# Three value projections between the RWKV projections, and other memory for the retention's tiles

## The chip, the cores and the metric

The kernel runs on one core of one Trainium2 chip. The metric is the device time of one execution, in microseconds (us). The kernel before the change takes 1903.56 us, the median of 3 runs (1901.87 to 1906.99).

## What is computed

A decoder block on 1024 tokens of width 1024, all in float32. One projection of the normalised input feeds two token mixers and two gates; the mixers' outputs are merged, and a feed-forward part with a short convolution follows:

```python
hn = rms_norm(h, norm_mix_pre);  p = hn @ w_in
p_rw, p_ret, g_rw, g_ret = split(p)        # 1792, 3072, 1024, 1024 columns
y_rw  = rwkv7_mixer(p_rw, ...)             # r, k, v, decay, a, g; a recurrence per head
y_ret = retention_mixer(p_ret, positions)  # q, k, v, g; 8 heads, chunks of 128 tokens
merged = sigmoid(g_rw) * (y_rw @ w_branch_rw) + sigmoid(g_ret) * (y_ret @ w_branch_ret)
h = h + rms_norm(merged @ w_out, norm_mix_post)
h = h + rms_norm(conv_ffn(rms_norm(h, norm_ffn_pre), ...), norm_ffn_post)
```

The retention works chunk by chunk: scores of a chunk against itself under a decay mask, plus the query times a carried state, then a normalisation per head and a product with the gate.

## The kernel before

A framework orders the instructions: it takes the program in the order written as the priority, simulates the engines, and gives each engine a fixed list. What is written inside a `high_priority` block counts as written 500 instructions earlier; weight loads (`load_w`) and the emptying of PSUM are in such blocks. Memory comes from pools that are stacked on the left or the right end of SBUF. A pool that is opened where another was closed waits, tile by tile, for the last use of what lay there.

Every large product is done as three matmuls per 128 rows (`mm3`): both operands are split into a high and a low float32r part, and high x high, high x low and low x high are added up in PSUM. `load_w` brings in 512 KB of weights on SP's queue, casts the high part on ScalarE (line 211) and subtracts for the low part on VectorE when a running count is divisible by 3, otherwise on GpSimd (line 216).

The 54 column tiles of `w_in` (128 columns each, 1024 tokens in two halves of 512) fall into two kinds. Tiles 0 to 13 are the RWKV ones: `rw_tiles` and `rw_tile` (lines 339 to 367) project them, and VectorE and ScalarE mix each with its shifted self. Four come first; then a loop over i = 0 to 3 (lines 402 to 464) computes decay and `a` from two small products (`p_lw`, `p_a`), scans, scales k and r, and writes the packed operands of the recurrence to DRAM (`L_d`). The others are the side tiles: `qk_pair` projects q and k with their rotation (tiles 14 to 21), `side_tile(i)` v (22 to 29), the retention's gate (30 to 37) and the two merge gates (38 to 53). Both put their result through the PSUM tag "a" (two banks, which the RWKV tiles use too) and the buffer `ot` into the DRAM tensor `pj_d`:

```python
w = load_w(wch[i], 8)
for hf in range(2):
    ps = psA.tile([128, 512], F32, tag="a", name="ps_side")
    proj(w, ps, hf)                                   # 24 matmuls of 512 columns
    with tc.high_priority(offset=WPRIO):
        ot = gp.tile([128, 512], F32, tag="ot", name="ot")
        if i < 30:
            S.copy(ot, ps)
```

In program order there follow: the recurrence, 8 chunks (lines 576 to 762), its memory (`rc`, `r1`, `r2`) on the right; the side tiles up to 37; the retention (`first_stage` of chunk j+1, then `second_stage` of chunk j); the side tiles 38 to 53; the first product of the RWKV branch (`ps_b0`, 8 x 12 matmuls, lines 881 to 897), from `yrw_d` and the gates in `pj_d`; then the merge for two halves of the tokens, whose second product (`ps_b`, lines 998 to 999) takes the retention's output `yret_d`.

The retention's pool `t2` is opened on the right when the recurrence's pools are closed. A chunk's q, k, v and gate come in one load `zvg` (1.5 MB, two buffers, SP's queue); `vt`, `sm`, `kt_`, `R`, `on` and `yr` have two buffers each, and `yr` goes out in one store on ScalarE's queue. `t2` is closed behind the retention; `h2`, `np` (the first product's gates `gt0`, tag "pr") are opened then in its place, and `mr` (the product's inputs) on the left. The rotation's tables `cosT` and `sinT` lie in `hp`, as does the projections' input `hn`.

Of the kernel before, what the change touches and what calls it, by code (L numbers as in the profile page):

```python
# [158 lines left out]
def body(tc, nc, xT, xN, pos, wch, wbrw, wbret, wout, wup, wdn, w2a2, gw2, rows, vecs, consts0, consts1, out):  # L159
# [3 lines left out]
    @contextmanager  # L163
    def tile_pool(**kw):
        with tc.tile_pool(**kw) as pool:
            yield Lines(pool)

    with ctx:
# [101 lines left out]
        cosT = hp.tile([128, T], F32, name="cosT")  # L270
        sinT = hp.tile([128, T], F32, name="sinT")
# [44 lines left out]
        def rbh(hf):  # L316
            return rbT[:, 512 * hf:512 * hf + 512]

# [7 lines left out]
        with pctx, tile_pool(name="p1", bufs=1, reuse_waits="tile", side="right") as p1:  # L326
# [57 lines left out]
            rt, rg, k0, r0 = rw_tiles([(12, "v_"), (13, "cs"), (4, "k_"), (0, "r_")], w0)  # L384
            nc.sync.dma_start(cst[1], consts1)
# [16 lines left out]
            for i in range(4):  # L402
# [58 lines left out]
                for c in range(2):  # L461

                    o = 2048 + 128 * i + 64 * (1 - c)
                    nc.scalar.dma_start(L_d[:, :, o:o + 64].rearrange("j p t -> p j t"), v_.rearrange(jct, c=2, t=64)[:, :, c, :])

# [34 lines left out]


        pj_d = dp.tile([40, 128, T], F32, name="pj_d")

        def qk_pair(m):

            ws = [load_w(wch[14 + 2 * m + e], 8) for e in range(2)]
            for hf in range(2):
                h_ = slice(hf * 512, (hf + 1) * 512)
                ab = []
                for e in range(2):  # L510
                    ps = psA.tile([128, 512], F32, tag="a", name="ps_side")
                    proj(ws[e], ps, hf)
                    with tc.high_priority(offset=WPRIO):
                        t = gp.tile([128, 512], F32, tag=f"qk{e}", name="qk", bufs=1)
                        S.copy(t, ps)
                    ab.append(t)
                a_, b_ = ab
                o1 = gp.tile([128, 512], F32, tag="ot", name="ot")
                t2 = gp.tile([128, 512], F32, tag="rt", name="rot", bufs=1)
                G.tensor_tensor(out=o1, in0=a_, in1=cosT[:, h_], op=ALU.mult)  # L520
                V.tensor_tensor(out=t2, in0=b_, in1=sinT[:, h_], op=ALU.mult)
                V.tensor_tensor(out=o1, in0=o1, in1=t2, op=ALU.subtract)
                G.tensor_tensor(out=a_, in0=a_, in1=sinT[:, h_], op=ALU.mult)
                V.tensor_tensor(out=b_, in0=b_, in1=cosT[:, h_], op=ALU.mult)
                o2 = gp.tile([128, 512], F32, tag="ot", name="ot")
                V.tensor_tensor(out=o2, in0=b_, in1=a_, op=ALU.add)
                dst = pj_d[2 * m:2 * m + 2, :, h_].rearrange("i (e z d) t -> z (i e) d t", e=2, z=2)
                for z, o in enumerate((o1, o2)):
                    for n in range(4):
                        nc.scalar.dma_start(dst[z, n], o[32 * n:32 * n + 32, :])  # L530

        def side_tile(i):

            w = load_w(wch[i], 8)
            for hf in range(2):
                ps = psA.tile([128, 512], F32, tag="a", name="ps_side")
                proj(w, ps, hf)
                with tc.high_priority(offset=WPRIO):
                    ot = gp.tile([128, 512], F32, tag="ot", name="ot")
                    if i < 30:  # L540
                        S.copy(ot, ps)
                    elif i < 38:
                        V.tensor_tensor(out=ps, in0=ps, in1=rbh(hf), op=ALU.mult)
# [222 lines left out]
        for i in range(22, 38):  # L766
            side_tile(i)
# [535 lines left out]
```

## Time and profile before

| | us |
|---|---|
| median of 3 runs | 1903.56 |
| the profiled execution | 1905.19 |
| its span, first to last instruction | 1903.4 |
| TensorE busy | 1789.1 |
| VectorE busy | 1194.9 |
| GpSimd busy | 697.7 |
| ScalarE busy | 648.5 |

The mean granted clock of TensorE was 0.979 of full speed. Busy time counts each engine's instructions, with overlaps of one engine counted once; a matmul's own time (0.39 us) is longer than the distance to the next, for they run pipelined. Stretches below are counted from the first instruction.

### The profile page before, as it was taken

To read this page: it belongs to the slowest core of one execution; us is meant where nothing else is said; L and a number is where in the kernel's file an instruction comes from. 1 tells how busy PE (TensorE), PEld (TensorE's weight loads), DVE (VectorE), ACT (ScalarE), POOL (GpSimd) and SP (SyncE) were. 2 spreads that over 40 slices of the span, in tenths; PEclk is the share of its full clock that TensorE was granted. 3 is DMA by queue.
4 is the path that set the end of the run, shared out by engine and by line. 5 is a ranking of instruction groups with operands and counts; after the bars stand their busy time and mean duration, and the time that the engine had idled before them with its cause. 6 is when DMAs were issued, how large, how long until landed. Compare 5 with 4: busy or idle time off the path is not lost.

```text
span 1903.4 us, 27398 instructions
## 1 busy us (share of the span) xinstructions
PE 1789.1 (94%) x10610; PEld 1451.0 (76%) x10610; DVE 1194.9 (63%) x2052; ACT 648.5 (34%) x993; POOL 697.7 (37%) x507
## 2 busy tenths in 40 slices
PE   8779999999999999999999999788999999999996
PEld 7657778788777778878788777666777777778885
DVE  4786584755666634663445828879888887753413
ACT  6543211111111112332443434543443444443330
POOL 1344523312212111111564744746455445222533
PEclk9989989999999999999999999899999999999998
DMA  8333532433333225555743726332222222674531
GB/s 289 90 106 100 191 81 68 133 90 94 109 93 111 69 78 162 154 178 172 238 155 119 241 89 194 133 132 104 80 78 78 78 78 75 213 221 142 178 102 44
DMA packets 202691, 244.44 MB, mean 128 GB/s; under 512 B 60993, under 2 KB 136257, under 8 KB 201537
## 3 DMA queue, kind: packets, MB, share of 16 engines
q1 hardware_dynamic: 125712, 171.11, 29.0%
q10 hardware_dynamic: 76848, 71.59, 11.5%
q8 instruction: 83, 1.36, 0.3%
q14 instruction: 48, 0.39, 0.1%
HBM read 177.10 MB, written 65.54 MB: 127 GB/s over the span
## 4 chain that ended last, share of the span: by engine, by line
PE 53%; DVE 23%; DMA 9%; issue 5%; ACT 5%; POOL 3%; ACTq 1%; SPq 0%; DVEq 0%; POOLq 0%
PE ps_side L223 7%; PE ps_side L222 7%; PE ps_side L224 7%; DVE u_f L1059 4%; PE ps_dn L224 3%; PE ps_dn L223 3%; PE ps_dn L222 3%; DVE u_f L1061 2%; POOL w_lo L1153 2%; DVE w_sa L1157 2%; DVE w_sa L1156 1%; PE ps_o L223 1%; PE ps_o L224 1%; PE ps_o L222 1%; PE ps_b L224 1%
## 5 line engine op out<-in xcount | busy, mean ns | idle before, releaser
L216 POOL TENSOR_TENSOR w_lo<-w_st,w_hi 128x1024 fp32r<-128x1024 f32 (+2 forms) x107 | 251.0, 2347 | 483.0 <-ACT w_hi L211 156.1
L211 ACT CAST w_hi<-w_st 128x1024 fp32r<-128x1024 f32 (+2 forms) x162 | 161.7, 999 | 396.6 <-PE ps_side L223 123.0
L223 PE MATMUL ps_side<-hnl,w_hi 128*128 128x512 f32 x640 | 256.2, 400 | 0.0
L222 PE MATMUL ps_side<-hnh,w_hi 128*128 128x512 f32 x640 | 256.0, 400 | 0.0
L224 PE MATMUL ps_side<-hnh,w_lo 128*128 128x512 f32 x640 | 255.1, 399 | 0.0
L222 PEld LDWEIGHTS ps_side<-hnh,w_hi 128*128 128x128 f32 x640 | 121.1, 189 | 26.9 <-issue 1.5
L223 PEld LDWEIGHTS ps_side<-hnl,w_hi 128*128 128x128 f32 x640 | 121.2, 189 | 26.4 <-issue 1.5
L224 PEld LDWEIGHTS ps_side<-hnh,w_lo 128*128 128x128 f32 x640 | 121.1, 189 | 26.3 <-issue 0.8
L216 DVE TENSOR_TENSOR w_lo<-w_st,w_hi 128x1024 fp32r<-128x1024 f32 (+1 forms) x55 | 71.9, 1307 | 83.6 <-ACT w_hi L211 39.6
L1059 DVE SCALAR_TENSOR_TENSOR u_f<-ub,vct,u_f 128x512 f32<-128x512 f32 x88 | 102.7, 1171 | 8.2 <-ACT u_f L1058 8.1
L1153 POOL TENSOR_TENSOR w_lo<-w_st,w_hi 128x512 fp32r<-128x512 f32 (+1 forms) x53 | 105.9, 2021 | 1.4 <-issue 1.4
L1058 ACT ACTIVATE u_f<-ub,vct 128x512 f32<-128x512 f32 x76 | 59.9, 813 | 123.6 <-DVE ub L1191 102.3
L222 PE MATMUL ps_rw<-hnh,w_hi 128*128 128x512 f32 (+1 forms) x224 | 86.9, 388 | 13.4 <-ACT hnh L287 7.2
L223 PE MATMUL ps_rw<-hnl,w_hi 128*128 128x512 f32 (+1 forms) x224 | 86.1, 385 | 0.3 <-DVE hnl L288 0.3
L224 PE MATMUL ps_rw<-hnh,w_lo 128*128 128x512 f32 (+1 forms) x208 | 79.7, 384 | 0.0
L224 PE MATMUL ps_b<-y_hi,w_lo 128*128 128x512 f32 x192 | 75.7, 395 | 2.9 <-DVE w_lo L216 2.0
L222 PE MATMUL ps_b<-y_hi,w_hi 128*128 128x512 f32 x192 | 75.9, 395 | 0.2 <-ACT w_hi L211 0.2
L223 PE MATMUL ps_b<-y_lo,w_hi 128*128 128x512 f32 x192 | 75.4, 393 | 0.0
L1061 DVE SCALAR_TENSOR_TENSOR u_f<-ub,vct,u_f 128x512 f32<-128x512 f32 x88 | 72.6, 843 | 0.2
L222 PE MATMUL ps_dn<-f_k,w_hi 128*128 128x512 f32 (+1 forms) x198 | 72.4, 366 | 0.0
L224 PE MATMUL ps_dn<-f_k,w_lo 128*128 128x512 f32 (+1 forms) x198 | 72.4, 366 | 0.0
L223 PE MATMUL ps_dn<-f_k,w_hi 128*128 128x512 f32 (+1 forms) x198 | 72.2, 366 | 0.0
(419 smaller groups left out, 4376.5 us busy)
## 6 DMA issues: line engine op xcount, KB each, us to landing
w_st<-in_wup_dram SPq DMA_DIRECT2D x54, 512.0 KB, 3.5
w_st<-in_wch_dram SPq DMA_DIRECT2D x52, 512.0 KB, 4.0
w_st<-in_wdn_dram SPq DMA_DIRECT2D x38, 512.0 KB, 4.1
pj_d<-ot ACTq DMA_DIRECT2D x64, 256.0 KB, 2.2
zvg<-pj_d SPq DMA_DIRECT2D x8, 1536.0 KB, 9.0
f_d<-u_f ACTq DMA_DIRECT2D x44, 256.0 KB, 2.1
L<-L_d SPq DMA_DIRECT2D x8, 1344.0 KB, 5.8
gt<-pj_d SPq DMA_DIRECT2D x32, 256.0 KB, 4.2
```

The lines of the kernel that those rows point to most:

```text
L211: S.copy(hi, st)
L216: eng.tensor_tensor(out=lo, in0=st, in1=hi, op=ALU.subtract)
L222: PE.matmul(ps, wh, xh, start=first and a == 0, stop=False, skip_group_check=skip)
L223: PE.matmul(ps, wh, xl, start=False, stop=False, skip_group_check=skip)
L224: PE.matmul(ps, wl, xh, start=False, stop=last and a == n - 1, skip_group_check=skip)
L1058: S.activation(u, src, AF.Identity, bias=VC("cb")[:, i:i + 1], scale=VC("cw2")[:, i:i + 1])
L1059: V.scalar_tensor_tensor(out=u, in0=ub[:, 1:513], scalar=VC("cw1")[:, i:i + 1], in1=u, op0=ALU.mult, op1=ALU.add)
L1061: V.scalar_tensor_tensor(out=u, in0=ub[:, 0:512], scalar=VC("cw0")[:, i:i + 1], in1=u, op0=ALU.mult, op1=ALU.add)
L1153: eng.tensor_tensor(out=w[1][:, ks, :], in0=src, in1=w[0][:, ks, :], op=ALU.subtract)
L1156: V.tensor_tensor(out=sa[:, lh, :], in0=st2[:, lh, :], in1=st2[:, rh_, :], op=ALU.add)
L1157: V.tensor_tensor(out=sa[:, rh_, :], in0=st1[:, lh, :], in1=st2[:, lh, :], op=ALU.subtract)
```

## The change

The definitions of `qk_pair`, `side_tile` and `pj_d` move, word for word, ahead of the RWKV projections. `side_tile(22)` is written behind the first four RWKV tiles, `side_tile(23)` at the end of the loop's pass i = 0, `side_tile(24)` at the end of pass i = 1; the loop behind the recurrence starts at 25. `h2` and `np` are opened ahead of the retention, `t2` (small vectors only from now on) and `mr` on the left. The retention's large tiles go to slots of other pools: q, k, gate, `vt` and `sm` into the 16 tags of `h2`; v into the memory of `cosT` and `sinT`, over which `on` is then written; `kt_` and `R` into tags of `gp`. The gate's tile takes the product in place of `yr`. The framework's DMA scratch shrinks to 1024 bytes.

```diff
-        cosT = hp.tile([128, T], F32, name="cosT")
-        sinT = hp.tile([128, T], F32, name="sinT")
+        cosT = hp.tile([128, T], F32, tag="tb0", name="cosT")
+        sinT = hp.tile([128, T], F32, tag="tb1", name="sinT")
...
             rt, rg, k0, r0 = rw_tiles([(12, "v_"), (13, "cs"), (4, "k_"), (0, "r_")], w0)
+            n_early = (1, 1, 1, 0, 0)
+            i_early = iter(range(22, 22 + sum(n_early)))
+            for _ in range(n_early[0]):
+                side_tile(next(i_early))
...
+                for _ in range(n_early[1 + i]):
+                    side_tile(next(i_early))
...
-        for i in range(22, 38):
+        for i in range(22 + sum(n_early), 38):
             side_tile(i)
...
-        tctx = ExitStack()
-        t2 = tctx.enter_context(tile_pool(name="t2", bufs=2, reuse_waits="tile", side="right"))
+        h2 = ctx.enter_context(tile_pool(name="h2", bufs=1, reuse_waits="tile", side="right"))
+        nctx = ExitStack()
+        np_ = nctx.enter_context(tile_pool(name="np", bufs=2, reuse_waits="tile", side="right"))
+        t2 = hctx.enter_context(tile_pool(name="t2", bufs=2, reuse_waits="tile"))
+        mr = hctx.enter_context(tile_pool(name="mr", bufs=1, reuse_waits="tile"))
+
+        def slots(j, n, name):
+            return [h2.tile([128, 4, 128], F32, tag=f"b0{z}{4 * (j % 2) + n}", name=name) for z in "hl"]
...
-                zvg = t2.tile([128, 24, 128], F32, name="zvg")
-                nc.sync.dma_start(zvg, pj_d[0:24, :, tk].rearrange("i p t -> p i t"))
-            Z, vc, sg = (zvg[:, 8 * n:8 * n + 8, :] for n in range(3))
-            vt = t2.tile([128, 8, 128], F32, name="vt")
+                Z = slots(j, 0, "Z")
+                vc = hp.tile([128, 8, 128], F32, tag=f"tb{j % 2}", name="vc")
+                sg = slots(j, 1, "sg")
+                for z in range(2):
+                    nc.sync.dma_start(Z[z], pj_d[4 * z:4 * z + 4, :, tk].rearrange("i p t -> p i t"))
+                nc.sync.dma_start(vc, pj_d[8:16, :, tk].rearrange("i p t -> p i t"))
+                for z in range(2):
+                    nc.sync.dma_start(sg[z], pj_d[16:24, :, tk].rearrange("(i e) p t -> e p i t", e=2)[z])
+            vt = slots(j, 2, "vt")
...
-            sm = t2.tile([128, 8, 128], F32, name="sm")
+            sm = slots(j, 3, "sm")
...
-                kt_ = t2.tile([128, 4, 128], F32, name="kt_")
+                kt_ = gp.tile([128, 4, 128], F32, tag="rt", name="kt_", bufs=1)
...
-                R = t2.tile([128, 4, 128], F32, name="R")
+                R = gp.tile([128, 4, 128], F32, tag=f"qk{j % 2}", name="R", bufs=1)
...
-            return Z, vt, sm, sg, Rj
+            return Z, vc, vt, sm, sg, Rj
-        def second_stage(j, Z, vt, sm, sg, Rj):
-            on = t2.tile([128, 8, 128], F32, name="on")
+        def second_stage(j, Z, on, vt, sm, sg, Rj):
...
-            yr = t2.tile([128, 4, 2, 128], F32, name="yr")
...
-                V.tensor_tensor(out=yr[:, :, e, :], in0=p_y.rearrange(h4, h=4),
-                                in1=sg.rearrange("p (i e) t -> p i e t", e=2)[:, :, e, :], op=ALU.mult)
-            nc.scalar.dma_start(yret_d[:, :, j * 128:(j + 1) * 128].rearrange("(i e) p t -> p i e t", e=2), yr)
+                V.tensor_tensor(out=sg[e], in0=p_y.rearrange(h4, h=4), in1=sg[e], op=ALU.mult)
+                nc.scalar.dma_start(yret_d[:, :, j * 128:(j + 1) * 128].rearrange("(i e) p t -> e p i t", e=2)[e], sg[e])
...
-        tctx.close()
         for i in range(38, 54):
             side_tile(i)
...
-    nc = bacc.Bacc("TRN2", target_bir_lowering=False, num_devices=1)
+    nc = bacc.Bacc("TRN2", target_bir_lowering=False, num_devices=1, dynamic_dma_scratch_size=1024)
```

## Rows read from the trace of the kernel before

**Rows 1.** The page: the span, and busy us of each engine (share, instructions).

```profile
span 1903.4 us, 27398 instructions
PE 1789.1 (94%) x10610; PEld 1451.0 (76%) x10610; DVE 1194.9 (63%) x2052; ACT 648.5 (34%) x993; POOL 697.7 (37%) x507
```

**Rows 2.** Stretches: us, busy us by engine (instructions), clock, DMA share, GB/s.

```profile
57.00:212.70 155.70, 137.64 (x568) 106.84 (x569) 115.12 (x104) 67.57 (x82) 72.34 (x65) 0.93 0.35 107
90.00:104.00 14.00, 3.08 (x9) 1.77 (x8) 13.26 (x9) 3.86 (x6) 7.58 (x7) 0.66 0.43 137
146.00:182.00 36.00, 34.16 (x150) 26.83 (x148) 24.93 (x22) 14.92 (x18) 19.02 (x13) 1.00 0.31 97
182.00:212.70 30.70, 29.48 (x128) 23.25 (x129) 20.45 (x18) 10.15 (x12) 14.78 (x14) 1.00 0.41 127
212.70:720.00 507.30, 502.22 (x4603) 402.77 (x4602) 298.25 (x790) 92.54 (x145) 118.60 (x112) 0.99 0.34 99
720.00:876.00 156.00, 155.35 (x1018) 126.60 (x1017) 94.11 (x320) 45.63 (x97) 21.65 (x13) 1.00 0.52 160
905.40:926.50 21.10, 18.14 (x71) 13.45 (x70) 10.40 (x12) 8.21 (x14) 11.42 (x8) 0.94 0.76 263
```

**Rows 3.** Waits of TensorE, 57 to 212.7 us: total, times, longest.

```profile
PE p_a L414 <- ACT ta L416: 7.3, 1, 7.3
PE ps_rw L222 <- DVE v__314 L362: 5.0, 1, 5.0
PE p_lw L410 <- ACT th L412: 3.6, 1, 3.6
```

**Rows 4.** Timeline of TensorE, 83 to 105 us: start, duration, instruction.

```profile
85.67 0.40 PE L223 MATMUL ps_rw<-hnl,w_hi 128*128 128x512 f32 x1
90.46 0.39 PE L223 MATMUL ps_rw<-hnl,w_hi 128*128 128x512 f32 x1
104.22 0.63 PE L222 MATMUL ps_rw<-hnh,w_hi 128*128 128x512 f32 x1
```

**Rows 5.** Stretches, instructions of the side tiles' PSUM tile alone.

```profile
212.70:720.00 507.30, 350.01 (x1410) 261.25 (x1410) 28.87 (x42) 28.21 (x48) 0.99 0.34 99
720.00:876.00 156.00, 94.75 (x382) 69.43 (x381) 11.02 (x16) 0.00 (x0) 1.00 0.52 160
876.00:905.40 29.40, 29.40 (x131) 24.21 (x129) 3.45 (x5) 0.00 (x0) 1.00 0.64 214
```

**Rows 6.** Groups by line, 57 to 212.7 us: count, busy us, mean ns.

```profile
L216 POOL TENSOR_TENSOR w_lo<-w_st,w_hi 128x1024 fp32r<-128x1024 f32 x7 | 19.4, 2779 | 7.7 <-PE ps_rw L224 7.7
L211 ACT CAST w_hi<-w_st 128x1024 fp32r<-128x1024 f32 x10 | 10.4, 1044 | 23.0 <-DVE BKp L447 11.9 <-PE ps_rw L223 11.1
L216 DVE TENSOR_TENSOR w_lo<-w_st,w_hi 128x1024 fp32r<-128x1024 f32 x3 | 3.6, 1213 | 0.0
```

**Rows 7.** The side tiles' output tile: duration ns min/median/max, first and last start.

```profile
L541 ACT COPY ot<-ps_side x16: 571/584/587, 349.7 to 490.4; 128x512 f32<-128x512 f32 x16
```

**Rows 8.** Timeline of all engines, 96 to 101 us.

```profile
96.33 1.22 DVE L446 TENSOR_TENSOR k__316<-ta,k__316 128x1024 f32<-128x1024 f32 x1
97.55 2.35 POOL L216 TENSOR_TENSOR w_lo<-w_st,w_hi 128x1024 fp32r<-128x1024 f32 x1
97.65 3.33 DVE L447 TENSOR_TENSOR BKp<-k__316,th 128x1024 f32<-128x1024 f32 x1
```

**Rows 9.** Waits of SP's DMA queue, 700 to 930 us.

```profile
SPq L783 <- DVE yr L863: 52.4, 6, 16.6
```

**Rows 10.** DMA issues: count, KB each, median us to landing.

```profile
zvg<-pj_d SPq DMA_DIRECT2D x8, 1536.0 KB, 9.0
yret_d<-yr ACTq DMA_DIRECT2D x8, 512.0 KB, 7.1
yt<-yret_d ACTq DMA_DIRECT2D x16, 256.0 KB, 4.6
```

**Rows 11.** Instructions on the retention's output in DRAM.

```profile
L973 ACTq DMA_DIRECT2D yt<-yret_d x16: 326/326/572, 906.5 to 982.4; - x16
```

More of the change, by code (lines that the diff above doesn't have):

```diff
@@ L317, in rbh, with qk_pair @@
             return rbT[:, 512 * hf:512 * hf + 512]
+        pj_d = dp.tile([40, 128, T], F32, name="pj_d")
+        def qk_pair(m):
+            ws = [load_w(wch[14 + 2 * m + e], 8) for e in range(2)]
+            for hf in range(2):
+                h_ = slice(hf * 512, (hf + 1) * 512)
+                ab = []
+                for e in range(2):
+                    ps = psA.tile([128, 512], F32, tag="a", name="ps_side")
+                    proj(ws[e], ps, hf)
+                    with tc.high_priority(offset=WPRIO):
+                        t = gp.tile([128, 512], F32, tag=f"qk{e}", name="qk", bufs=1)
+                        S.copy(t, ps)
+                    ab.append(t)
+                a_, b_ = ab
+                o1 = gp.tile([128, 512], F32, tag="ot", name="ot")
+                t2 = gp.tile([128, 512], F32, tag="rt", name="rot", bufs=1)
+                G.tensor_tensor(out=o1, in0=a_, in1=cosT[:, h_], op=ALU.mult)
+                V.tensor_tensor(out=t2, in0=b_, in1=sinT[:, h_], op=ALU.mult)
+                V.tensor_tensor(out=o1, in0=o1, in1=t2, op=ALU.subtract)
+                G.tensor_tensor(out=a_, in0=a_, in1=sinT[:, h_], op=ALU.mult)
+                V.tensor_tensor(out=b_, in0=b_, in1=cosT[:, h_], op=ALU.mult)
+                o2 = gp.tile([128, 512], F32, tag="ot", name="ot")
+                V.tensor_tensor(out=o2, in0=b_, in1=a_, op=ALU.add)
+                dst = pj_d[2 * m:2 * m + 2, :, h_].rearrange("i (e z d) t -> z (i e) d t", e=2, z=2)
+                for z, o in enumerate((o1, o2)):
+                    for n in range(4):
+                        nc.scalar.dma_start(dst[z, n], o[32 * n:32 * n + 32, :])
@@ new lines, in side_tile @@
+        def side_tile(i):
+            w = load_w(wch[i], 8)
+            for hf in range(2):
+                ps = psA.tile([128, 512], F32, tag="a", name="ps_side")
+                proj(w, ps, hf)
+                with tc.high_priority(offset=WPRIO):
+                    ot = gp.tile([128, 512], F32, tag="ot", name="ot")
+                    if i < 30:
+                        S.copy(ot, ps)
+                    elif i < 38:
+                        V.tensor_tensor(out=ps, in0=ps, in1=rbh(hf), op=ALU.mult)
+                        S.activation(ot, ps, AF.Tanh, scale=0.5)
+                        V.scalar_tensor_tensor(out=ot, in0=ot, scalar=1.0, in1=ps, op0=ALU.add, op1=ALU.mult)
+                    else:
+                        V.tensor_tensor(out=ot, in0=ps, in1=rbh(hf), op=ALU.mult)
+                        S.activation(ot, ot, AF.Tanh, scale=0.5)
+                    nc.scalar.dma_start(pj_d[i - 14, :, hf * 512:(hf + 1) * 512], ot)
@@ L499, in body @@
                 V.tensor_tensor(out=dst, in0=dst, in1=rbT, op=ALU.mult)
[L502 to L543, printed above, removed]
-                        S.activation(ot, ps, AF.Tanh, scale=0.5)
-                        V.scalar_tensor_tensor(out=ot, in0=ot, scalar=1.0, in1=ps, op0=ALU.add, op1=ALU.mult)
-                    else:
-                        V.tensor_tensor(out=ot, in0=ps, in1=rbh(hf), op=ALU.mult)
-                        S.activation(ot, ot, AF.Tanh, scale=0.5)
-                    nc.scalar.dma_start(pj_d[i - 14, :, hf * 512:(hf + 1) * 512], ot)
@@ L799, in first_stage @@
                     lo = 64 * e
[L800 removed]
+                    PE.matmul(p_ss[e][:, i * 128:(i + 1) * 128], Z[1][lo:lo + 64, i, :], Z[0][lo:lo + 64, i, :],
                               start=True, stop=True)
             for e in range(2):
[L803 removed]
+                V.tensor_tensor(out=sm[e], in0=p_ss[e].rearrange(h4, h=4), in1=rmask, op=ALU.mult)
             Rj = R
```

16 lines of the change are left out of this document (5 added, 11 removed).

## The prediction

> **What bounds the kernel now.** I began with the page's busy times, then cut the span into stages with the stretch table, then asked in each stage what TensorE waits for. TensorE is busy 1789.1 of 1903.4 us [rows 1]; the stages tell where the rest lies [rows 2]. From 212.7 to 720 us (the RWKV recurrence) it is busy 502.22 of 507.30 us, from 720 to 876 us (the retention) 155.35 of 156.00: there the side tiles (the projections of q, k, v and the gates) fill what the two mixers leave open, and every matmul taken out shortens the stage, as long as other fillers remain. The stage before, 57 to 212.7 us, holds the RWKV projections without side tiles: busy 137.64 of 155.70 us at a granted clock of 0.93. The reader should see there that TensorE is not the bound: from 90 to 104 us it is busy 3.08 of 14 us while VectorE is busy 13.26, and the granted clock averages 0.66 of 2.4 GHz, so a part of the stretch ran at 1.2 GHz [rows 2]. The waits name the cause: 7.3 us for `ta`, 3.6 us for `th`, and, ending where the stage begins, 5.0 us for a PSUM bank that VectorE empties [rows 3].
>
> **The pace of a tile.** From 85.67 to 90.46 us, 21 matmuls of 512 columns start one behind the other: 4.79 us, or 0.228 us each [rows 4]. A side tile has 2 x 8 x 3 = 48 of them, 10.9 us; the three moved ones have 144, 32.8 us. The stage from 57 to 212.7 us holds 568 matmuls [rows 2], all 512 wide, so 129.5 us of work in 155.7: 26.2 us are free, the time lost to the half-rate clock among them.
>
> **Step 1, three tiles leave the full stage.** Taking 144 matmuls out of the stages that TensorE fills takes 32.8 us off them if fillers don't run out. The side tiles' matmuls lie 1410 in the recurrence, 382 in the retention and 131 behind it [rows 5]. If the recurrence and the retention keep their gaps, they want 1792 fillers; 37 tiles have 1776. The 16 that are short (3.6 us) come from the first branch product, 8 x 12 = 96 matmuls, which has operands of its own from now on. So I cost running short at nothing; the cover is that product, and without it the price is 3.6 us. What is late next, behind the retention, is the branch's second product (rival 2).
>
> **Step 2, three tiles enter the projection stage.** The stage then holds 712 matmuls, 162.3 us at full pace. Lower bound of its growth: 6.6 us, if no hole is left. Upper bound: 32.8 us, if VectorE's chain sets the pace and the tiles only push it along. Between them I take the filling that this stage reaches where it runs best: from 146 to 212.7 us there are 150 + 128 matmuls, 63.4 us of work in 66.7, or 0.950 [rows 2]. 162.3 / 0.950 is 170.8 us, 15.1 more than now. The big hole takes the first tile: TensorE's dense run ends just behind 90.46 us and resumes at 104.22 [rows 4], and a tile of 10.9 us placed ahead of that shifts the blocked `p_a` matmul to where `ta` is free. The other two tiles lie where only some 13 us of small holes and half-rate clock are left, so they mostly lengthen the stage. Steps 1 and 2: 32.8 - 15.1 = 17.7 us gained, with bounds 0 and 26.2.
>
> **What each moved tile brings with it.** A weight load on the SP queue, a cast on ScalarE (1.04 us), a subtraction on GpSimd (2.78 us on average) or VectorE (1.21 us) [rows 6], two copies of 0.58 us out of PSUM on ScalarE [rows 7] and two DMAs on ScalarE's queue. The engine of the subtraction goes by a count, so the load order shifts it: of the three extra ones, two fall to GpSimd and one to VectorE. ScalarE is busy 67.57 of 155.7 us, GpSimd 72.34, VectorE 115.12 [rows 2]; 3 x 2.2, 2 x 2.8 and 1.2 us fit under all of them while TensorE sets the pace, and the growth taken in step 2 (8.5 us above its floor) holds them. In the 14 us where VectorE has no room the cover is gone: there one subtraction costs its 1.2 us. The evacuations need no VectorE, and each frees its bank of the two that the RWKV tiles also use. The copy waits for its matmuls in ScalarE's queue, and `ta`, `th` and the casts stand behind it; half a tile is 5.5 us, so one badly placed copy costs at most that.
>
> A row speaks for a higher price. The `BKp` product (line 447) takes 3.33 us when it starts 0.10 us behind a weight subtraction on GpSimd, while the product of the same size on line 446 took 1.22 us just before it [rows 8]. The Trainium skill, SBUF — State Buffer, section "Who interferes with whom", says that a VectorE instruction with two SBUF inputs contends with a GpSimd instruction that reads SBUF; by its words the two added GpSimd subtractions would each block one VectorE product. By that rule, with 2.1 us for each from the trace, the gain of 17.7 us would be 13.5; as VectorE is the bound only in the first 50 us of the stage, I leave it at 17.7.
>
> **Step 3, the retention's tiles.** Its matmuls, DVE passes and bytes stay the same. Per chunk, one load on the SP queue becomes five (q, k, v, and two for the gate); one store on ScalarE's queue becomes two. That is 4 x 8 more issues on SP and 8 on ScalarE, beside a full TensorE: nothing, and q and k come earlier. Upper bound: the first chunk's loads, which no earlier chunk hides, land one behind the other at the 4.6 us of a 256 KB load, 5 x 4.6 = 23.0 us instead of the 9.0 of the one load [rows 10], 14.0 us once; but side tiles fill TensorE meanwhile. The wait added is the gate's load for chunk j+2, which goes into memory that the store of chunk j still reads; behind it in SP's queue stand weight loads, for which the splits and then TensorE wait (rival 3). The wait it replaces is there now: the loads stand 52.4 us in six waits for `yr` [rows 9], at no cost to TensorE. A gain from the earlier q and k could only come out of the 0.65 us in which TensorE idles there [rows 2]. I take 0.
>
> **Step 4, the first product.** From 905.4 to 926.5 us, 71 matmuls (16.2 us) run in 21.1 us: 4.9 us open [rows 2], while the splits of `yt` and of the branch weights fall together. With `h2`, `np` and `mr` opened ahead of the retention, the product's operands and gates can be fetched before it ends. Bounds 0 and 4.9 us; I take the middle, 2.4, because the `yt` loads still start only when the projections' input is released (the first at 906.5 us [rows 11]) and still meet the same engines.
>
> The smaller DMA scratch I cost at nothing: the program issues every DMA from SP's and ScalarE's queues, none from GpSimd's, before and after.
>
> **Sum.** 17.7 + 2.4 = 20.1 us. The profiled execution took 1905.19 us (span 1903.4 and 1.8 around it), 1.6 over the median of 1903.56: 1885.1 by its own time, 1883.5 by the median. Own range of this case: 1873 to 1893, from every hole filled (rival 4) to half the gain.
>
> **Rivals.** (1) VectorE sets the projection stage: 115.12 of 155.7 us busy, 13.26 of 14 in the big hole. Then the tiles only push the chain along, the stage grows by 32.8 us, and the time stays at 1901 to 1904. Against it: behind 146 us TensorE fills 0.95 of the time, and the tiles' own evacuations avoid VectorE. Chance 0.12. (2) The fillers run out earlier than counted, and the first product is used up inside the retention. Then the second product waits for the retention's last store (7.1 us to landing), its load (4.6 us) [rows 10], a cast and a split (1.04 and 1.21 us at most [rows 6]): 13.9 us; 6.2 us of the gain remain, 1897. For it: the account is short by 16 matmuls. Against it: the first 512 tokens' loads need only chunks 0 to 3, and less filling makes the retention itself shorter. Chance 0.12. (3) Slower: the gate's load of chunks 2 to 7 holds SP until the store has landed, and the weights behind it come late. Price: 6 x 7.1 = 42.6 us, less 20.1, so 1926. It decides once a block of SP exceeds what two staged weights cover, about 19.5 us (156 us over 8 tiles [rows 2, 5]); the longest wait of the loads now is 16.6 us [rows 9], under it, and TensorE idles 0.65 us in the whole retention. Chance 0.08. (4) Everything fills: 26.2 + 4.9 = 31.1 us, 1872.5. For it: the half-rate clock returns with the holes closed. Chance 0.08. The forecast keeps 0.60.
>
> **How the numbers follow.** This kernel's measurement tells about 0.3% (5.7 us) from no change, so faster means under 1897.9. Faster: 0.60 + 0.08, half of rival 2 (it lies on the line) and a quarter of rival 1 (a push that is not quite whole): 0.77. Same: the rest of these two, 0.15. Slower: 0.08. The range 1871 to 1902 holds the forecast, rival 2, half of rival 4 and some of rival 1, about 8 in 10.
>
> **What would show it.** Right: side tiles from about 64 us on; no hole over 5 us between 64 us and the first recurrence matmul; the granted clock of the stage near 0.98; the RWKV projections' end at about 228 us instead of 212.7; about 29 tiles' worth of side matmuls still in the recurrence; the last side matmul near 886 us instead of 905. Wrong: the hole at 90 us still there beside the new tiles (rival 1, step 2); TensorE idle behind the retention for over 5 us (rival 2); weight loads late behind the gate's load (rival 3).

## The result and the profile after

The changed kernel takes 1915.7 us, the median of 8 runs (1907.5 to 1920.7), beside 1902.0 us for the kernel before in the same session (8 runs): a ratio of 1.0059, 95% interval 1.0043 to 1.0075. It is slower by 0.4 to 0.75%; the forecast was 1883.5 us, faster.

The page of the changed kernel, profiled in an execution of 1913.03 us; it answers to [rows 1]:

```profile
span 1910.9 us, 27467 instructions
PE 1790.3 (94%) x10610; PEld 1455.9 (76%) x10610; DVE 1192.6 (62%) x2052; ACT 647.3 (34%) x993; POOL 699.7 (37%) x507
```

The work is the same on every engine; the span is 7.5 us longer. Stretches of the changed kernel, columns as in [rows 2]; its projections end at 233.2 us and its side tiles at 886.1:

```profile
57.00:233.90 176.90, 165.64 (x706) 130.93 (x705) 110.89 (x100) 73.30 (x90) 78.15 (x65) 0.98 0.36 112
90.00:104.00 14.00, 9.19 (x30) 7.21 (x31) 10.53 (x8) 5.59 (x8) 9.78 (x6) 0.76 0.63 197
233.90:742.00 508.10, 498.64 (x4592) 400.25 (x4591) 304.60 (x797) 93.42 (x146) 122.76 (x114) 0.99 0.36 105
742.00:886.30 144.30, 139.80 (x883) 116.12 (x883) 72.84 (x248) 38.53 (x82) 18.71 (x13) 0.99 0.52 163
886.30:925.00 38.70, 36.72 (x230) 30.57 (x228) 23.46 (x79) 11.57 (x26) 7.69 (x10) 1.00 0.45 130
925.00:950.00 25.00, 17.56 (x63) 13.32 (x62) 10.84 (x10) 8.77 (x15) 11.76 (x7) 0.86 0.70 241
```

The first column behind the bounds is the stretch's length, the next TensorE's busy time. The projection stage is fuller than before, at a clock of 0.98 instead of 0.93. What is new lies behind: TensorE is idle 9.5 us in the recurrence (508.10 - 498.64), 4.5 and 2.0 in the retention, 7.4 behind it. Added to the 11.3 of the projection stage that is 34.6 us. The same sum before is 18.1 + 5.1 + 0.65 + 3.0 = 26.8 [rows 2]. So 7.9 us of idle time came in, of which, by estimate, the better clock of the projection stage gives back 5.4 (137.64 us / 568 matmuls before, 165.64 / 706 now: 7.7 ns each, 706 times).

The ends of three stages, first in the kernel before, then in the changed one: the RWKV projections (`ps_rw`), the side tiles (`ps_side`) and the branch products of the merge (`ps_b`). The two times in a row are its first and last start:

```profile
L224 PE MATMUL ps_rw<-hnh,w_lo x208: 280/389/629, 8.5 to 212.0; 128*128 128x512 f32 x88, 128*128 128x256 f32 x16
L224 PE MATMUL ps_side<-hnh,w_lo x640: 387/389/632, 213.2 to 905.3; 128*128 128x512 f32 x160
L224 PE MATMUL ps_b<-y_hi,w_lo x192: 387/389/637, 906.0 to 1091.3; 128*128 128x512 f32 x192
```

```profile
L224 PE MATMUL ps_rw<-hnh,w_lo x208: 280/389/416, 8.5 to 233.2; 128*128 128x512 f32 x88, 128*128 128x256 f32 x16
L224 PE MATMUL ps_side<-hnh,w_lo x640: 387/389/628, 62.1 to 886.1; 128*128 128x512 f32 x160
L224 PE MATMUL ps_b<-y_hi,w_lo x192: 387/389/628, 887.0 to 1093.9; 128*128 128x512 f32 x192
```

The merge's second product ends 2.6 us later than before (1093.9 and 1091.3), and 4.9 us more are lost between there and the end of the span (817.0 us now, 812.1 before), in stages whose lines the change leaves as they are. Why those take longer is not shown.

The side tiles' own matmuls by stretch; they answer to [rows 5]:

```profile
57.00:233.90 176.90, 36.63 (x145) 28.75 (x146) 0.00 (x0) 3.47 (x6) 0.98 0.36 112
233.90:742.00 508.10, 345.16 (x1395) 257.11 (x1395) 32.99 (x48) 24.75 (x42) 0.99 0.36 105
742.00:925.00 183.00, 93.36 (x382) 70.50 (x382) 11.01 (x16) 0.00 (x0) 0.99 0.51 156
```

The recurrence took 1395 of them where it took 1410, the retention 382 where it took 382. What is gone are the 131 behind the retention. Fillers left, but the two mixers did not get shorter. Where the retention stands is seen in the transposes `p_y`, eight at the end of each chunk. The changed kernel (first and last start, us):

```profile
L882 PE MATMUL p_y<-cst,vc x64: 270/272/332, 781.4 to 924.9; 128*128 128x128 f32 x64
```

and the kernel before:

```profile
L862 PE MATMUL p_y<-cst,on x64: 270/273/330, 752.7 to 874.5; 128*128 128x128 f32 x64
```

The retention ends 50.4 us later. 21.2 of these are the later end of the projections (233.2 against 212.0), 1.3 the recurrence, 6.2 the first chunk (up to its `p_y`), and 21.7 the retention itself, which lasts 143.5 us from first to last `p_y` instead of 121.8. Waits of TensorE in the changed kernel, 742 to 960 us (total, times, longest):

```profile
PE ps_b L222 <- ACT y_hi L992: 7.1, 2, 4.1
PE p_v L813 <- DMA vc<-pj_d: 6.5, 5, 2.0
```

The first is the merge's second product, which waits for the retention's output; the second is the retention waiting for its v tiles. Neither wait of such length was there before.

The kernel before and the changed one were each profiled a second time.

> The kernel before, unchanged, profiled a second time, to see which of its stage ends repeat. Theory that the stages' ends are set by the list of instructions and repeat: projections end at 212 us and the retention at 870 to 880 us again, and what differs between executions lies in many small waits. Rival: single large waits come and go from one execution to the next, and a stage end moves by over 8 us.

> The changed kernel, unchanged, profiled a second time. Path theory: projections end at 233 us, the retention's chunks come every 20 us, the retention ends at 918 to 930 us, the last side matmul is at about 886 us, and TensorE waits behind it for the merge's inputs by over 5 us again. Rival: the first profile's retention was a single bad execution; here it ends under 910 us with no wait of over 5 us behind it.

They took 1902.6 and 1909.5 us. The second profile before:

```profile
L862 PE MATMUL p_y<-cst,on x64: 270/273/330, 754.5 to 875.5; 128*128 128x128 f32 x64
```

the second one after:

```profile
L882 PE MATMUL p_y<-cst,vc x64: 270/272/332, 782.8 to 924.1; 128*128 128x128 f32 x64
```

and its waits of TensorE, 742 to 960 us:

```profile
PE ps_b L222 <- ACT y_hi L992: 7.6, 2, 4.1
PE p_v L813 <- DMA vc<-pj_d: 6.0, 5, 2.5
```

The ends of the stages repeat to within 2 us, and so do the two waits. The profiles put the changed kernel 7 and 8 us behind, the timings 8 to 14 (the interval). From the last `ps_b` matmul to the end the second pair differs by 3.8 us (813.0 and 809.2), and two executions of one kernel by 3 to 4 us. What the timings show beyond the profiles is in no profile and stays open.

### The profile page after: what moved, and what is told of

Same layout as the page of the kernel before. It is cut to its first block, busy times and chain, and to the rows that moved or that the text cites. A ratio compares the mean times of both kernels' runs of the same rounds, so it can differ in the third digit from the quotient of the medians.

```text
span 1910.9 us, 27467 instructions
## 1 busy us (share of the span) xinstructions
PE 1790.3 (94%) x10610; PEld 1455.9 (76%) x10610; DVE 1192.6 (62%) x2052; ACT 647.3 (34%) x993; POOL 699.7 (37%) x507
## 4 chain that ended last, share of the span: by engine, by line
PE 42%; DVE 23%; DMA 12%; issue 5%; POOL 3%; ACT 3%; SPq 1%; ACTq 0%; DVEq 0%; POOLq 0%
PE ps_side L222 5%; PE ps_side L223 5%; PE ps_side L224 5%; DVE u_f L1073 4%; PE ps_dn L224 3%; PE ps_dn L222 3%; PE ps_dn L223 3%; POOL w_lo L1167 2%; DVE u_f L1075 2%; DVE xprod L633 2%; DMA vc<-pj_d 2%; DVE w_sa L1171 2%; DMA w_st<-in_wup_dram 2%; DVE w_sa L1170 2%; PE ps_o L223 1%
## 5 line engine op out<-in xcount | busy, mean ns | idle before, releaser
L222 PE MATMUL ps_dn<-f_k,w_hi 128*128 128x512 f32 (+1 forms) x198 | 72.4, 366 | 0.0
L224 PE MATMUL ps_dn<-f_hl,w_lo 128*128 128x512 f32 x176 | 66.1, 398 | 6.6 <-DVE w_lo L216 6.6
```

The source lines that it names most:

```text
L222: PE.matmul(ps, wh, xh, start=first and a == 0, stop=False, skip_group_check=skip)
L224: PE.matmul(ps, wl, xh, start=False, stop=last and a == n - 1, skip_group_check=skip)
```

## The experiments

The first theory was that the tiles alone gain their 20 us and that only the retention's new memory costs. The theory that took its place, called path theory in the expectations: projections, recurrence, retention and the merge's loads are one chain. Its end was hidden behind side tiles; the change pushes its head back and takes away what hid its end. All kernels in one table: the projections' end (last start of `ps_rw`), first and last start of `p_y` and the time between, the last side matmul, the median, and the ratio to the kernel before with its interval.

| kernel | proj. end | p_y | length | side end | median us | ratio |
|---|---|---|---|---|---|---|
| before | 212.0 | 752.7 to 874.5 | 121.8 | 905.3 | 1902.0 | |
| changed | 233.2 | 781.4 to 924.9 | 143.5 | 886.1 | 1915.7 | 1.0043 to 1.0075 |
| tiles alone | 236.0 | 790.4 to 910.2 | 119.8 | 909.2 | 1922.0 | 1.0083 to 1.0126 |
| memory alone | 212.4 | 761.7 to 899.4 | 137.7 | 908.4 | 1912.0 | 1.0030 to 1.0068 |
| second stage first | 233.4 | 776.4 to 935.5 | 159.1 | 875.4 | 1923.6 | 1.0091 to 1.0128 |
| own `on` | 234.2 | 786.0 to 918.2 | 132.2 | 895.7 | 1902.1 | 0.9977 to 1.0015 |
| own `yr` | 235.7 | 790.0 to 924.4 | 134.4 | 901.4 | 1905.9 | 1.0009 to 1.0046 |
| own `on`, `yr` | 236.4 | 784.0 to 915.9 | 131.9 | 893.4 | 1901.8 | 0.9967 to 1.0006 |
| own `on`, two `kt_` | 232.6 | 780.1 to 912.3 | 132.2 | 889.8 | 1902.9 | 0.9986 to 1.0024 |
| one tile, memory before | 216.7 | 756.2 to 884.0 | 127.8 | 896.2 | 1905.7 | 1.0008 to 1.0034 |
| one tile, memory changed | 216.6 | 758.9 to 892.7 | 133.8 | 892.7 | 1900.0 | 0.9972 to 1.0009 |
| one tile, own `on`, `yr` | 217.3 | 754.5 to 882.9 | 128.4 | 891.2 | 1901.4 | 0.9993 to 1.0017 |
| no tile, own `on`, `yr` | 209.6 | 755.1 to 886.3 | 131.2 | 905.4 | 1907.5 | 1.0025 to 1.0055 |

A stage end is that of one execution, a median that of 6 to 12. Executions of one kernel lie up to 17 us apart, so a profile's span and a median can differ by several us. The profiles of the tiles alone, own `on` and own `yr` fell on the longest execution of their kernel (1929.3, 1908.3 and 1916.3 us); those of the second stage first, one tile with the memory changed, one tile with own `on` and `yr`, and no tile fell on the shortest (1917.5, 1895.2, 1893.4 and 1905.3).

**The tiles alone.** The kernel before, with the helpers and three tiles moved, and nothing else.

```diff
...
             rt, rg, k0, r0 = rw_tiles([(12, "v_"), (13, "cs"), (4, "k_"), (0, "r_")], w0)
+            n_early = (1, 1, 1, 0, 0)
+            i_early = iter(range(22, 22 + sum(n_early)))
...
-        for i in range(22, 38):
+        for i in range(22 + sum(n_early), 38):
```

> The kernel before, with the three tiles moved and nothing else: the retention keeps its pool on the right, its one load per chunk, its own on and yr. Theory (the retention's new memory lengthens its chunks, the tiles are worth what was forecast): projections end near 233 us as in the changed kernel, transposes p_y of two chunks 17 us apart as before, side tiles end near 886, second branch product starts near 910; 1884 to 1890 us, ratio about 0.992. Rival (the tiles themselves cost it: fillers run out, or the longer projection stage is not paid back): chunks or the gap behind the retention lengthen here too, 1902 to 1915 us, ratio 1.000 or more.

It was slower still: 1922.0 us, over the 1884 to 1890 us of the first theory, which fell with this run, and over the rival's 1902 to 1915 us too. Stretches of this kernel (columns as above):

```profile
236.00:755.00 519.00, 506.59 (x4592) 405.90 (x4591) 305.63 (x796) 92.11 (x144) 119.25 (x113) 0.97 0.33 96
755.00:870.00 115.00, 115.00 (x760) 93.80 (x760) 69.00 (x238) 30.93 (x65) 14.71 (x9) 1.00 0.58 174
910.00:930.00 20.00, 1.66 (x7) 0.70 (x4) 6.88 (x8) 6.22 (x11) 8.12 (x6) 0.61 1.00 354
```

and its waits of TensorE from 742 to 960 us:

```profile
PE ps_b L222 <- ACT y_hi L893: 16.5, 1, 16.5
```

The retention itself is as quick as before (119.8 us), but begins 38 us later: 24 by the projections, some 11 by the recurrence in this long execution. It ends at 910.2 us with the last side tile beside it (909.2), and nothing is left to hide the loads of the branch's first product: TensorE works 1.66 of 20 us, at a mean clock of 0.61. This kernel shows what the first product's own memory is good for: in the changed one that product starts at 886.4 us, right behind the side tiles.

**The memory alone.** The changed kernel with `n_early` set to (0, 0, 0, 0, 0).

> The changed kernel with no tile moved: only the memory and the loads of the retention, and the pools opened early. Theory: chunks 20 us apart instead of 17, the retention ends near 903 instead of 875 us; but the side tiles then still run to 905 and the first product to about 926, so that the delay is hidden: 1900 to 1908 us, ratio 0.999 to 1.003. Rival (the memory is innocent): chunks 17 us apart, ratio 1.000 or below.

Slower too, by 0.3 to 0.7%, with no tile moved: the retention lasts 137.7 us and ends 24.9 us later, 9 us ahead of the side tiles:

```profile
L882 PE MATMUL p_y<-cst,vc x64: 270/272/330, 761.7 to 899.4; 128*128 128x128 f32 x64
L224 PE MATMUL ps_side<-hnh,w_lo x640: 387/389/628, 213.6 to 908.4; 128*128 128x512 f32 x160
```

So the two halves of the change each cost time by themselves. But the expectation had the late retention hidden, and with it 1900 to 1908 us. It is hidden, and the time is 1912.0. In the profiles (executions of 1914.4 and 1905.2 us) the last side matmul comes 3.1 us later than before, the last `ps_b` matmul 4.4 (1095.7 and 1091.3), and 4.8 more are lost behind that. Path theory does not account for this run.

**Another order.** The theory was that the next chunk's first stage, written ahead of the second, held the second back.

```diff
-            cur, nxt = nxt, (first_stage(j + 1) if j < NJ - 1 else None)
+            cur = nxt
             second_stage(j, *cur)
+            nxt = first_stage(j + 1) if j < NJ - 1 else None
```

> The changed kernel, but in the retention's loop second_stage(j) is written ahead of first_stage(j+1), so that it has precedence. Theory (the early loads let the scores and transposes of chunk j+2 go ahead of the products of chunk j+1 in TensorE's list): chunk spacing falls from 20 to about 17 us, retention ends near 900, 1885 to 1895 us, ratio 0.99 to 0.996. Rival A (the loop is long because v is loaded only when the transposes of on have left its memory, and because SP waits for stores): spacing stays at 20 us, ratio 1.004 to 1.008. Rival B (tiles): ratio 1.004 to 1.008 with any spacing.

The retention got longer still (159.1 us), and the kernel with it (1923.6 us): this order is not the cause, and it was better as it stood.

**What holds the retention.** In the changed kernel `on` is written over v. The load of v for chunk j+2 then has to wait until `p_y` of chunk j has read `on`, and not only until `p_v` has read v. Timeline of SP's queue in the changed kernel, around the end of a chunk (start, duration):

```profile
823.16 0.36 SPq L803 DMA_DIRECT2D Z<-pj_d  x1
823.93 0.36 SPq L804 DMA_DIRECT2D vc<-pj_d  x1
```

and TensorE's (in brackets the idle time before, and its cause):

```profile
822.97 0.93 PE L882 MATMUL p_y<-cst,vc 128*128 128x128 f32 x7
829.33 0.66 PE L813 MATMUL p_v<-cst,vc 128*128 128x128 f32 x4 [1.59 <-DMA vc<-pj_d]
```

The load of v goes out as the last `p_y` ends, at 823.9 us, and TensorE, whose list has a fixed order, stands at the next `p_v` until it has landed. Waits of SP's queue in the changed kernel, 740 to 930 us:

```profile
SPq L806 <- DMA yret_d<-sg: 31.3, 11, 6.5
...
SPq L804 <- PE p_y L882: 11.2, 5, 7.6
```

So two edits, apart and together: `on` in a tile of its own in `t2`, and the gate's product in one, `yr`. (Together, and in the versions with one tile and none, `on` has one buffer instead of two.)

```diff
-        def second_stage(j, Z, on, vt, sm, sg, Rj):
+        def second_stage(j, Z, vt, sm, sg, Rj):
+            on = t2.tile([128, 8, 128], F32, name="on")
...
```

> The changed kernel, but on has a tile of its own (two buffers in t2), so that the load of v for chunk j+2 waits only for the transposes of v, not for those of on. Theory A (the retention is longer because v comes late: TensorE waits 6.5 us for it and its list stands still behind): spacing of the chunks' output transposes from 20.4 back to about 17 us, the retention ends near 900 us instead of 925, 1892 to 1900 us, ratio 0.995 to 0.999. Theory B (the gate's loads wait for stores and hold SP): spacing stays 20, ratio 1.005 to 1.009.

```diff
+                yr = t2.tile([128, 4, 128], F32, tag=f"yr{e}", name="yr")
-                V.tensor_tensor(out=sg[e], in0=p_y.rearrange(h4, h=4), in1=sg[e], op=ALU.mult)
+                V.tensor_tensor(out=yr, in0=p_y.rearrange(h4, h=4), in1=sg[e], op=ALU.mult)
...
```

> The changed kernel, but the product with the gate goes to a tile of its own (two buffers in t2), so that the gate's load for chunk j+2 doesn't wait for the store of chunk j. Theory A: spacing stays near 20 us, ratio 1.005 to 1.009. Theory B: spacing about 17 us, retention ends near 900, ratio 0.995 to 0.999.

> The changed kernel with both: on (one buffer) and the product with the gate in tiles of their own. Theories A and B: spacing about 17 us and ratio 0.993 to 0.998. If the spacing stays at 20 us, neither wait is the cause, and what is left is the split of the load, the single buffer of kt_, or the order of the list.

All issues of the v load (first and last start), first in the changed kernel:

```profile
L804 SPq DMA_DIRECT2D vc<-pj_d x8: 359/360/580, 441.5 to 888.8; - x8
```

then with `on` in its own tile:

```profile
L804 SPq DMA_DIRECT2D vc<-pj_d x8: 359/371/1385, 442.0 to 841.2; - x8
```

The last v is fetched 47.6 us earlier, near the 842.8 us of the last `zvg` load before; TensorE's wait for `vc` is gone, the retention lasts 11.3 us less, and the kernel takes as long as the kernel before (1902.1 us; with both, 1901.8). The longest wait of TensorE that is left from 742 to 960 us:

```profile
PE ps_b L222 <- ACT w_hi L211: 3.6, 1, 3.6
```

So the wait for v is shown as a cause. Theory A itself went too far: its chunks every 17 us and 1892 to 1900 us did not come (18.9 us, 1902.1). The gate's tile costs less, but not nothing: with `yr` alone 1905.9 us and a retention of 134.4. The two do not add up: 11.3 and 9.1 us of the retention apart, 11.6 together. And the time stops at that of the kernel before although the merge is ahead: in the profiles the last `ps_b` matmul starts at 1089.2 us with own `on` and 1087.4 with both (before: 1091.3), but the rest then takes 817.2 and 816.0 us (before: 812.1). Why is open.

The remaining 10 us of the retention (132 against 122) are not explained. They are no fixed price of the memory: with one tile moved the mended retention lasts 128.4 us beside 127.8 with the memory before. One candidate was the single buffer of the transposed keys:

```diff
-                kt_ = gp.tile([128, 4, 128], F32, tag="rt", name="kt_", bufs=1)
+                kt_ = t2.tile([128, 4, 128], F32, name="kt_")
```

> The changed kernel (three tiles moved) with the normalised output in a tile of its own and, beside that, two buffers for the transposed keys instead of one. Theory that the single buffer of the transposed keys is what keeps the retention's chunks at 18.5 us with the normalised output mended: 17.5 us or less from chunk to chunk, the retention's end at about 911 us instead of 918, 1896 to 1900 us. Rival (the split loads, the order of the list or the fewer fillers set the rest): 18.2 us or more, 1900 to 1906 us.

The length stays at 132.2 us, some 18.9 from chunk to chunk: it was not this buffer. The five loads in place of one, the order of the list and the smaller DMA scratch remain, each untried by itself.

**How many tiles.** One tile (22) instead of three, with the memory before and with the changed one; then, with the changed memory mended, one tile and none.

```diff
-            n_early = (1, 1, 1, 0, 0)
+            n_early = (1, 0, 0, 0, 0)
```

> The kernel before with one tile moved, the first, behind the four first RWKV tiles; all else as before. If the big hole at 90 us takes it as the prediction says: projections end 0 to 4 us later than before (212 to 216), 7 to 11 us gained, 1891 to 1895 us, ratio 0.994 to 0.996. If VectorE's chain is only pushed along: projections end near 223, ratio 1.000.

> The changed kernel with one tile moved instead of three. Path theory (the end of the retention, which the projections' end pushes back, sets the merge's start once the fillers run out before it): projections end near 217 instead of 233 us, retention ends near 908 instead of 925, side tiles end near 896 instead of 886, merge's second product near 918; 1898 to 1906 us, ratio 0.998 to 1.002. Rival (only the retention's memory is at fault, the tiles gain what they should): fewer tiles gain less, 1920 to 1928 us, ratio 1.010 or more.

> The changed kernel with only the first tile moved, and the normalised output and the gate product in tiles of their own. Path theory: projections end at about 217 us, the retention ends at 882 to 888 us, the last side matmul comes at 894 to 897 us with no wait for the merge's inputs behind it; the side fillers and the path end nearly together, so the time is 1893 to 1900 us. Rival (the retention's end no longer matters once it lies near the fillers' end; only the tiles' pace counts): the same as with one tile and the memory unmended, 1900 us, within 2 us.

> The changed kernel with no tile moved, and the normalised output and the gate product in tiles of their own. It differs from the run with no tile moved only by these two tiles. Path theory: the projections end at 212 us as before the change, the retention's chunks come every 18 to 18.5 us instead of 19.5, the retention ends at 885 to 892 us instead of 899, under the last side matmul at about 906 us: hidden, so 1898 to 1906 us. Rival (something else in the new memory costs the 10 us, such as the five loads per chunk or the carried state's place): spacing still over 19 us and 1910 us or more.

One tile pushes the projections back by 4.7 us, three by 21. With the memory before, one tile is slower by 0.1 to 0.3% (1905.7 us); neither the 1891 to 1895 us of its expectation nor its rival's projections' end of 223 us came. With the memory as changed, the same tile brings back what the memory alone cost (1912.0): the retention's end (892.7 us) falls together with the last side matmul, and the 15 us of the changed kernel are gone: 1900.0 us, as path theory had it; the rival's 1920 us and more is out.

```profile
L882 PE MATMUL p_y<-cst,vc x64: 270/272/332, 758.9 to 892.7; 128*128 128x128 f32 x64
L224 PE MATMUL ps_side<-hnh,w_lo x640: 387/389/794, 62.2 to 892.7; 128*128 128x512 f32 x160
```

But once the path is hidden again nothing is gained beyond that: with the memory mended the retention ends 8 us ahead of the fillers, and the time is 1901.4, equal to the kernel before. That is the rival's figure and not the 1893 to 1900 us of path theory. With no tile, 1907.5 us lies 1.5 over what path theory gave, though the stage ends came as expected (886.3 and 905.4). In its profile, its shortest execution (1905.3 us), the last side matmul, the last `ps_b` matmul (1091.2) and the span (1903.4) are those of the kernel before, which was profiled in one of its longer ones (1905.2); where the 6 us of the timings come from is open. After the memory alone it is the second version in which a hidden retention is slower than the kernel before.

The one-tile version's first profile fell on its shortest execution, so it was profiled again.

> The kernel with one tile moved and the normalised output and the gate product in tiles of their own, profiled a second time; its first profile fell on its shortest execution (1893 us, median 1901). Path theory: the retention again ends at 880 to 888 us, ahead of the last side matmul, so that a longer time here comes from elsewhere than the merge's inputs. Rival: in a longer execution the retention ends behind the side matmuls and the merge waits for it.

It took 1900.65 us where the first took 1893.38. The stretch from 350 to 480 us, in the recurrence, in the first profile:

```profile
350.00:480.00 130.00, 128.66 (x1256) 104.14 (x1256) 74.62 (x226) 23.41 (x38) 25.14 (x24) 0.99 0.35 100
```

and in the second:

```profile
350.00:480.00 130.00, 127.12 (x1243) 102.85 (x1242) 71.40 (x212) 23.89 (x39) 22.85 (x24) 0.97 0.35 99
```

The projections end alike (217.3 and 217.1), then the recurrence comes out 8 us longer, with a lower clock and fewer matmuls in the same stretch; the retention (890.9) still ends ahead of the side tiles (899.2). What differs between these two executions lies in the recurrence, not at the merge.

**Where a tile is written.** The one-tile version with the tile at the second place, as shown, and at the third, with (0, 0, 1, 0, 0).

```diff
-            n_early = (1, 0, 0, 0, 0)
+            n_early = (0, 1, 0, 0, 0)
```

> One tile moved, but to the second place (behind the loop's pass 0) instead of the first; else as the one-tile version with the normalised output and the gate product in tiles of their own. Theory that the price of a tile in the projection stage follows from how many there are (the first fills the open time, whichever place it has): the projections' end moves from about 210 to 212 us without a tile to about 215 to 218 us, as with the tile at the first place (217). Rival (the place decides: the second place stands behind a PSUM bank that VectorE still holds, the 7.1 us wait in the changed kernel): 220 us or more, with such a wait on this tile's first matmul.

> One tile moved, to the third place (behind the loop's pass 1); else as the one-tile version. In the changed kernel that tile's matmuls lie from 147 to 160 us, where TensorE was nearly full before. Theory of the count: the projections' end at 215 to 218 us, since the hole at 90 us is still open but cannot be reached from there only if the place decides. Theory of the place: the whole 10.9 us of the tile are added, 220 to 223 us, and the hole at 90 us stays as it was in the kernel before (TensorE busy about 3 of 14 us).

The projections end at 217.1 and 218.4 us, as with the first place (217.1 and 217.3), in executions of 1903.9 and 1902.4 us. From the third place, where the tile's matmuls begin at 130 us, the hole at 90 us is less filled than from the second, yet the end is only 1.3 us later. The second place:

```profile
90.00:104.00 14.00, 10.01 (x32) 7.30 (x31) 10.85 (x6) 4.34 (x7) 6.94 (x5) 0.76 0.57 195
```

and the third:

```profile
90.00:104.00 14.00, 5.02 (x12) 3.54 (x13) 11.94 (x10) 6.55 (x9) 8.80 (x6) 0.63 0.55 187
```

So the place hardly matters for one tile. The price of the first is 4.2 to 7.7 us (216.6 against 212.4 with the memory changed, 217.3 against 209.6 with own `on` and `yr`), that of each further one (233.2 - 217.2) / 2 = 8.

## Why the prediction was wrong

**The pace** was right: where the stage is full now, from 104 to 182 us, 338 matmuls in 78 us are 0.231 us each, against 0.228.

**Step 1 failed, in its cover.** That "every matmul taken out shortens the stage" does not hold for the recurrence and the retention. The prediction's own count said so (they want 1792 fillers if they keep their gaps), but its sum took 32.8 us off. Only the 131 matmuls behind the retention, 29.9 us, could go, and they were what hid the end of the chain. The last side matmul came at 886.1 us, as forecast (886), and 29 tiles' worth lay in the recurrence (1395 / 48), as forecast; the time didn't follow. The cover that the prediction put in their place, the first product's 96 matmuls (21.9 us), would have reached: by its own numbers the retention ends at 874.5 + 15.1 = 889.6 us. It ended at 924.9, 35.3 us later than that: 6.1 from step 2, 1.3 from the recurrence, 6.2 from the first chunk and 21.7 from the retention, which step 3 put at 0.

**Step 2 had the direction, not the size:** 21.2 us instead of 15.1. The stage holds 706 matmuls, 161.0 us, in 176.9: filled to 0.91, not 0.95. From 104 to 182 us it is full; most of what is missing lies from 57 to 104, where 159 matmuls (36.3 us) take 47. The hole stayed beside the tiles, moved and shorter (TensorE in the changed kernel):

```profile
87.34 0.39 PE L470 MATMUL p_a<-LA,wll 128*128 128x512 f32 x1
94.81 0.79 PE L222 MATMUL ps_side<-hnh,w_hi 128*128 128x512 f32 x1 [7.08 <-DVE v__755 L412]
```

The wait is no longer for `ta` but for a PSUM bank: the second side tile stands 7.1 us until VectorE has emptied the bank of an RWKV tile, the same kind of wait as the 5.0 us of [rows 3]. A tile's own evacuations avoid VectorE, as the prediction said; the bank it needs does not. Rival 1 decided part of it. And the 21 us weigh more than in the sum, for they also move the whole chain behind.

**What each tile brings** was rightly small. VectorE's busy time in the stage fell from 115.12 us [rows 2] to 110.89. Its passes that lie beside a GpSimd read still take longer: in the changed kernel a `th` pass takes 0.68 us alone and 2.42 beside one, and `rk` takes 3.3 each time beside one. That agrees with the Trainium skill, SBUF — State Buffer, section "Who interferes with whom"; but there are 15 passes of over 1.9 us in the stage where there were 16, so no more were blocked, and the 4.2 us by that rule are not seen.

**Step 3 failed, and it is the largest term.** Its 0 rested on "side tiles fill TensorE meanwhile". The loads did come late, not by the first chunk's 14 us but chunk after chunk (the five waits of 11.2 us on SP's queue), by writing `on` over v, which the prediction mentions under the change and never prices. The retention grew by 21.7 us; with `on` in its own tile 11.3 of them are gone and the kernel is back at 1902.1 us, and some 10 are not explained. Rival 3's mechanism is visible (SP waits 31.3 us in 11 waits for the stores), but the longest is 6.5 us, no weight came late for TensorE between 742 and 925 us, and its 19.5 us were never reached. Still, the wait was not free: with own `yr` alone, which takes the product out of the gate's tile, the time fell from 1915.7 to 1905.9 us.

**Step 4 was right in kind:** the first product starts at 886.4 us, straight behind the side tiles; with the tiles alone TensorE stands idle there.

**Rival 2 is what happened, undervalued.** The first product was used up inside the retention, and the second waited, 7.1 us. Against it stood that the first 512 tokens need only chunks 0 to 3. ScalarE's timeline in the changed kernel shows why that does not help:

```profile
921.17 2.91 ACT L877 ACTIVATE vc<-p_o,nb,rh 128x128 f32<-128x128 f32 x8 [4.61 <-DVE nb L873]
923.77 0.34 ACTq L987 DMA_DIRECT2D yt<-yret_d  x1
928.57 0.62 ACT L992 CAST y_hi<-yt 128x512 fp32r<-128x512 f32 x1 [2.61 <-DVE sg L883]
```

The loads are issued from ScalarE's queue, behind the normalisation of the last chunk (before, the first went out at 906.5 us [rows 11]), and the first cast, by the bracket in its row, then stood 2.61 us more until the gate's product (`sg`) of the retention was done. Also wrong was "less filling makes the retention itself shorter". Its 1897 us kept the projected gain of 17.7; only the merge's wait was counted, and not that the chain arrives 50 us later.

**How the loss is shared.** By the runs each half costs by itself (tiles 16 to 24 us, memory 6 to 13, by the intervals), together 8 to 14. That the first product's memory takes back a part of what the tiles lose fits its start at 886.4 us, but no run has the tiles with this memory and the retention's old one. Mending `on` alone brings the changed kernel to the time of the kernel before; so does leaving two of the three tiles where they were. None of the versions is faster than the kernel before by more than its interval. So the runs show a main part of the loss, a retention that ends too late for its cover. Why even the mended versions gain nothing, and why the memory costs 6 to 13 us alone though its retention is hidden, stays open.

## What to carry to other kernels

Where low-priority work fills the gaps of a chain, as here, taking fillers out shortened nothing but the tail behind the chain. Before moving them, compare when the chain ends and when the fillers end (here 874.5 and 905.3 us, 31 us of cover): what is put ahead of the chain's head counts against that cover twice, once as delay and once as lost filling. And a result written over the buffer of a load ties the next load to the last reader of the result; look for it in the DMA queue's waits. A delay that is hidden by the stage ends need not be free: time the version, for the memory alone cost 0.3 to 0.7% with its end under cover.

## What the runs showed of the hardware

Two executions of one kernel (1893.4 and 1900.65 us) agree to 0.2 us at the projections' end and differ by 8 at the retention's first `p_y` (754.5 and 762.5), with a granted clock of 0.99 and 0.97 of full speed in 350 to 480 us. In 14 us where TensorE was busy 9.2 the clock averaged 0.76, in 20 us where it was busy 1.7 it averaged 0.61; full speed is 2.4 GHz, so a part of both ran at 1.2 GHz.
